# A hybrid decoder layer on one core: sixteen of the FFN's 22 inner tiles go through the down projection by seven block products, and small FFN operands move to PSUM

## The chip, the core and the metric

The kernel runs on one core of one Trainium2 chip. The metric is the device time in microseconds, as the median of several runs. Engines are named as in the profile: PE (matmul), PEld (its weight load), DVE (VectorE), ACT (ScalarE), POOL (GpSimd), SP (SyncE, which issues the DMAs here). Every engine works through its own queue in order.

## The reference, cut to what matters

The layer has a part that mixes tokens (three mixers, merged by gates) and a feed-forward part (FFN). The change lies in the FFN, with x of 1024 tokens by 1024 channels, D_FF = 2816, all float32:

```python
h = rms_norm(x, pre_ffn_norm)
u = causal_dwconv(h @ ffn_w_up, ffn_conv_w, ffn_conv_b)   # 1024 x 5632; three taps over time
gate, val = split(u)                                       # 2816 channels each
f = (gelu(gate, approximate=True) * val) @ ffn_w_down      # 2816 -> 1024
x = x + rms_norm(f, post_ffn_norm)
```

## The kernel before, in words

**Exact products by three matmuls.** Each float32 operand is kept as a rounded hi part (type fp32r) and the rest lo. A 128x128 block of weights times 128x512 of data is three matmuls: hi by hi, hi by lo, lo by hi. Making hi is a copy on ACT, making lo a subtraction on DVE or POOL. Data is channel by token: a tile has 128 channels and a half (512) of the tokens, h = 0 or 1.

**Seven block products.** Where a product is cut into 2x2 blocks, it can be made from seven products of sums of blocks in place of eight. The SSM part of the input projection and most of the up projection do this. `weights7` (L494 to L530) loads two tiles of 512 KB, makes the sums of weight blocks and splits them: four copies on ACT (L511, L520, L523, L525), eight operations on POOL (L512 to L526). `combos` makes the sums of the data blocks. `product` issues one of the seven, 12 matmuls.

**The FFN, up.** The FFN's 22 inner tiles are called f; each has a gate and a value tile (`u = 2f`, `2f+1`). The first `N_FIRST` = 4 are made plainly by halves in `up_half` (L1530), then `rhs` gets the sums of data blocks (L1571 to L1589), and 18 calls of `up_pair` (L1538) make one f each with 84 matmuls. Partial results collect in the PSUM banks x, y, z of a pool of six (`bank`); `snap` (L1512) copies the state of x to SBUF where a later step needs it. The second half of the value tile is the difference of two snapshots, s7 - s3, on POOL (L1555). `conv` runs the convolution over time in `E.conv` (L303 to L312): a scaled copy on ACT (L306), on DVE two shifted multiply-adds (L310) and, for h = 1, two narrow ones with the two columns at the edge kept from h = 0 (the `halo` tile, L308 and L312). GELU on ACT goes back into the gate's SBUF tile (L1524), `gated` (L1526) multiplies on DVE (L1527) and stores the tile to `m_d` in DRAM.

**The FFN, down.** `DOWN` lists six chunks of inner tiles: four, four, four, four, two, four. `m_split` (L1598) loads a tile of `m_d` into SBUF and splits it (ACT L1601, DVE L1602). `down` (L1604) does each of eight output tiles j by `fm_unit`, for both halves; the first chunk is copied to the 16 accumulator tiles `acc` by ACT (L1615), later ones are added by DVE (L1617). The last chunk is kept out of the loop: its weights and data are split ahead, and it is done column part by column part (`LAST`) with the final norm, the residual `x1` (two loads of 2 MB) and the output. The first chunk's splits are put into the last `up_pair` (`between`).

**Order.** A scheduler fixes each engine's order ahead of time from a model; tile pools make an instruction wait where a buffer is still in use. All loads and stores here are issued by SP in its order, so a load that waits for a buffer holds those behind it.

Of the kernel before, what the change touches and what calls it, by code (L numbers as in the profile page):

```python
# [33 lines left out]
C_ID, C_TI, C_MD, C_ME, C_TS, C_NT, C_SM = [128 * i for i in range(7)]  # L34
C_N = 8 * 128
# [57 lines left out]
def layout(a):  # L93
# [31 lines left out]
    for i, (c0, c1) in enumerate(TM_CHUNKS):  # L125
# [16 lines left out]

    dns = [units(dn[c * 128:(c + n) * 128], ar(DM)) for c, n in DOWN]
    out.update(
# [9 lines left out]
        wup=units(up, fch), **{f"wdn{i}": d for i, d in enumerate(dns)})  # L154
# [4 lines left out]
DOWN = [(0, 4), (4, 4), (8, 4), (12, 4), (16, 2), (18, 4)]  # L159
# [25 lines left out]
U_BUFS = 4  # L185
OSQ = 6

# [12 lines left out]
def trunk(ctx: ExitStack, tc: tile.TileContext, A: dict, outT: bass.AP, dbg=None):  # L200
# [24 lines left out]
    tab = cp.tile([128, C_N], F32, name="tab")  # L225
# [5 lines left out]
    ident = tab[:, C_ID:C_ID + 128]  # L231
    tri_i = tab[:, C_TI:C_TI + 128]
    rtab = cp.tile([128, 256], R32, name="rtab")
# [151 lines left out]
    nc.scalar.dma_start(ident, A["c_tab"][:, C_ID:C_ID + 128])  # L385
# [8 lines left out]
    nc.sync.dma_start(tab[:, 128:], A["c_tab"][:, 128:])  # L394
# [962 lines left out]
def tail_stage(nc, tc, es, env):  # L1357
# [49 lines left out]
    for n, (br_i, k0, nk, src) in enumerate(((2, 12, 4, "wb_nsa"), (1, 8, 4, "wb_sb"), (0, 0, 8, "wb_ssm"))):  # L1407
        if n == 2:
            yq = br.enter_context(tc.tile_pool(name="yq", side="right", reuse_waits="tile", bufs=8))
        ys = [load_y(k0 + k) for k in range(nk)]  # L1410
        for j in range(8):
            pss = fm_unit(psd, load_w(A[src][j], nk * 128), lambda k, h: ys[k][h], nk)
            e = (bt if n else E.bt0).tile([128, T], F32, name="ge")
            nc.sync.dma_start(e, E.g_d[(br_i * 8 + j) * 128:(br_i * 8 + j + 1) * 128, :])
            for h in range(2):
                b = e[:, hs(h)]
                d = b
                if n == 0:
                    d = part[h, j] = lo_t(F32)
                V.tensor_tensor(d, pss[h], b, op=OP.mult)  # L1420
                if n == 1:
                    P.tensor_tensor(part[h, j], part[h, j], b, op=OP.add)
                elif n == 2:
                    P.tensor_tensor(b, part[h, j], b, op=OP.add)
                    hi, lo = mix[h, j] = hi_t(), lo_t()
                    act(hi, b, AF.Copy)
                    V.tensor_tensor(lo, b, fl(hi), op=OP.subtract)
        if n == 0:
            E.both.close()
            E.st1.close()  # L1430
            psd = es.enter_context(tc.tile_pool(name="psd2", reuse_waits="tile", bufs=6, space=PSUM))
            psn = es.enter_context(tc.tile_pool(name="psn", reuse_waits="tile", bufs=2, space=PSUM))
# [74 lines left out]
    def bank():  # L1507
        return psd.tile([128, 512], F32, name="dense", tag="dense")

    def snap(ps):  # L1510
        s = up_.tile([128, 512], F32, name="snap", bufs=5)
        act(s, ps, AF.Copy)  # L1512
        return s

    m_d = E.scratch("m_d", [NFF * 128, T])

    def conv(u, h, ps, st):
# [19 lines left out]
    def up_pair(f, rhs, between=None):  # L1537

        st = {}
        w = E.weights7(wx, A["wup"][2 * f], A["wup"][2 * f + 1], 512)  # L1540
        x, y, z = bank(), bank(), bank()
        E.product(x, w, rhs, 1, True)
        s1 = snap(x)
        E.product(y, w, rhs, 2, True)
        V.tensor_tensor(y, y, s1, op=OP.add)
        conv(2 * f, 0, y, st)
        E.product(x, w, rhs, 6, False)
        s2 = snap(x)
# [6 lines left out]
        P.tensor_tensor(s7, s7, s3, op=OP.subtract)  # L1555
        E.product(z, w, rhs, 4, False)
        V.tensor_tensor(z, z, s2, op=OP.subtract)
# [14 lines left out]
    later = []  # L1572
    for k in range(4):
# [10 lines left out]
        later += [(5, k, t1, hi_t), (4, k, t4, lo_t)]  # L1584

    for q, k, t, place in sorted(later, key=lambda x: (-x[0], x[1])):
        rhs[q][k] = hi, lo = place(), x_t()
        act(hi, t, AF.Copy)
        V.tensor_tensor(lo, t, fl(hi), op=OP.subtract)  # L1589
# [3 lines left out]
    def m_tile(f, h, s):  # L1593
        t = x_t(F32) if s is None else up_.tile([128, 512], F32, name=f"u{s}")
        nc.sync.dma_start(t, m_d[f * 128:(f + 1) * 128, hs(h)])
        return t

    def m_split(f, h):  # L1598
        src = m_tile(f, h, None if f < DOWN[0][1] else f % 2)
        hi, lo = hi_t(), lo_t()  # L1600
        act(hi, src, AF.Copy)  # L1601
        V.tensor_tensor(lo, src, fl(hi), op=OP.subtract)  # L1602
        return hi, lo
# [4 lines left out]
    def down(ci, f0, nf, ms):  # L1608
        end = None
        for j in range(8):  # L1610
            pss = fm_unit(psd, load_w(A[f"wdn{ci}"][j], nf * 128), lambda k, h: ms[f0 + k, h], nf)
            for h, ps in enumerate(pss):
                a = acc[h][j]
                if ci == 0:
                    act(a, ps, AF.Copy)  # L1615
                else:
                    end = V.tensor_tensor(a, a, ps, op=OP.add)  # L1617
        return end
# [7 lines left out]
    tc.keep_in_program_order(nc.scalar.preload_act_table_set(E.TABLE))  # L1626
    for ci, (f0, nf) in enumerate(DOWN[:last]):
        if ci == 0:
            acc = [[x_t(F32) for _ in range(8)] for _ in range(2)]
        i = down(ci, f0, nf, m_chunk(f0, nf) if ci else ms0)  # L1630
        if ci == last - 2:
            late = i
# [5 lines left out]
    def w_split(j, place):  # L1638
        ws.append(load_w(A[f"wdn{last}"][j], 512, place, up_.tile([128, 512], F32, name="snap", bufs=5)))
# [17 lines left out]
    def norm_rows(ss, W):  # L1657
# [7 lines left out]
        rb = up_.tile([128, 512], F32, name="u1")  # L1665
# [15 lines left out]
    for s0, s1 in LAST:  # L1681
# [3 lines left out]
        ss = up_.tile([128, 512], F32, name="u0")  # L1685
        for j in range(8):
# [10 lines left out]
            else:  # L1697
                sq = up_.tile([128, 512], F32, name="snap", bufs=5)
# [24 lines left out]
```

## Time and profile before

| | us |
|---|---|
| median of three runs | 2294.1 |
| lowest and highest | 2286.16, 2295.38 |
| the profiled execution | 2297.28 |
| its span, first to last instruction | 2295.5 |
| mean granted clock of PE | 0.985 of full speed |

The span is the time from the first instruction to the last. The profile's times count from the span's start. The FFN's up projection begins shortly after 1600 us, and the down projection shortly after 2000. In a group of instructions, the columns are line, engine, operation, output and inputs by the program's names with their shapes, the count, then busy time in us, the mean of one in ns, and the idle time just before with what ended it. In a list of waits, the columns are who waited, for whom, and in us the total, the number of waits and the longest.

### The profile page before, as it was taken

The page shows a single profiled execution, that of the slowest core. Times are in us where ns is not written, and L with a number is a line of the kernel's source. Part 1 is how long each engine was busy: PE and PEld are TensorE (multiplying, and loading weights), DVE is VectorE, ACT ScalarE, POOL GpSimd, SP SyncE. Part 2 cuts the span into 40 slices and gives each one's busy share as a digit, 9 for nine tenths or more (in the row PEclk, how much of TensorE's full clock was granted, in tenths as well). Part 3 has the DMA queues.
Part 4 walks back from the last instruction along what each step waited for, and adds up shares of the span by engine and source line. Part 5 has one row for each costly group of instructions (what it writes and reads, how often), then busy time and mean ns, then how long its engine had stood idle before and what let it go on. Part 6 is the DMA issues. An engine that isn't in the chain of part 4 may idle for free.

```text
span 2295.5 us, 29758 instructions
## 1 busy us (share of the span) xinstructions
PE 2197.3 (96%) x10663; PEld 1755.3 (76%) x10663; DVE 1346.2 (59%) x2376; ACT 1164.9 (51%) x2185; POOL 1184.5 (52%) x853
## 2 busy tenths in 40 slices
PE   7999999998999999999999999999899999999997
PEld 7878889865665678878775678887678888878886
DVE  7765554268567526556536653359876777744346
ACT  6544443466756646667755421245545555553124
POOL 3676741246736733333347655446578888822213
PEclk9999999999999999999999999999999999999998
DMA  4233341320221011112253253334322222264212
GB/s 170 81 111 108 116 132 62 112 70 24 62 67 31 12 56 42 60 65 93 83 211 112 80 213 129 119 128 162 106 79 86 85 83 83 84 223 130 93 32 74
DMA packets 115349, 222.03 MB, mean 97 GB/s; under 512 B 28160, under 2 KB 42432, under 8 KB 115200
## 3 DMA queue, kind: packets, MB, share of 16 engines
q1 hardware_dynamic: 112608, 217.80, 28.0%
q10 hardware_dynamic: 2592, 2.32, 0.3%
q8 instruction: 84, 1.38, 0.2%
q14 instruction: 65, 0.53, 0.1%
HBM read 162.80 MB, written 57.28 MB: 96 GB/s over the span
## 4 chain that ended last, share of the span: by engine, by line
PE 77%; DVE 11%; ACT 5%; issue 3%; DMA 3%; POOL 2%; SPq 0%; DVEq 0%; ACTq 0%; POOLq 0%
PE dense L208 55%; PE ps_s L208 7%; PE ps_o L208 6%; PE ps_t L208 6%; PE ps_b L208 4%; POOL wlo L273 1%; DVE x L1484 1%; DVE mx L938 1%; DVE u L310 1%; DVE osq L1457 1%; DVE x L1589 1%; DMA wraw<-in_wdn 1%; DMA wraw<-in_wfm 0%; DVE x L1677 0%; DMA x<-in_xT 0%
## 5 line engine op out<-in xcount | busy, mean ns | idle before, releaser
L273 POOL TENSOR_TENSOR wlo<-wraw,whi 128x1024 fp32r<-128x1024 f32 (+2 forms) x134 | 266.5, 1989 | 444.1 <-ACT whi L272 435.4
L208 PE MATMUL dense<-hi,whi 128*128 128x512 f32 x816 | 308.2, 392 | 4.8 <-ACT whi L272 4.8
L208 PE MATMUL dense<-hi,wlo 128*128 128x512 f32 x752 | 289.3, 394 | 8.9 <-POOL wlo L273 7.9
L208 PE MATMUL dense<-lo,whi 128*128 128x512 f32 x688 | 269.3, 392 | 0.5 <-POOL lo L1497 0.5
L208 PE MATMUL dense<-h_hi,whi 128*128 128x512 f32 x656 | 263.8, 402 | 0.0
L208 PE MATMUL dense<-h_lo,whi 128*128 128x512 f32 x656 | 257.5, 393 | 0.0
L208 PE MATMUL dense<-h_hi,wlo 128*128 128x512 f32 x656 | 257.2, 392 | 0.0
L272 ACT ACTIVATE whi<-wraw 128x1024 fp32r<-128x1024 f32 (+2 forms) x134 | 116.1, 867 | 277.4 <-PE dense L208 228.8
L976 POOL TENSOR_TENSOR wT_lo<-wT,wT_hi 128x512 fp32r<-128x512 f32 x132 | 168.5, 1288 | 101.3 <-ACT wT_hi L975 93.2
L208 PEld LDWEIGHTS dense<-hi,whi 128*128 128x128 f32 x816 | 154.2, 189 | 39.5 <-ACT whi L272 6.9
L208 PE MATMUL dense<-x,uhi 128*128 128x512 f32 x552 | 177.3, 392 | 3.9 <-ACT x L584 2.4
L208 PEld LDWEIGHTS dense<-hi,wlo 128*128 128x128 f32 x752 | 142.1, 189 | 41.7 <-POOL wlo L273 10.4
L208 PEld LDWEIGHTS dense<-lo,whi 128*128 128x128 f32 x688 | 130.0, 189 | 28.6 <-POOL lo L1497 1.4
L208 PEld LDWEIGHTS dense<-h_hi,wlo 128*128 128x128 f32 x656 | 123.7, 189 | 26.7
L208 PEld LDWEIGHTS dense<-h_hi,whi 128*128 128x128 f32 x656 | 124.4, 190 | 23.8
L208 PEld LDWEIGHTS dense<-h_lo,whi 128*128 128x128 f32 x656 | 124.3, 189 | 22.5
L1180 POOL TENSOR_TENSOR s_lo<-sa,s_hi 128x512 fp32r<-128x512 f32 (+2 forms) x48 | 53.5, 1115 | 152.1 <-ACT s_hi L1179 152.1
L938 DVE TENSOR_REDUCE mx<-ps_t 128x1 f32<-128x384 f32 (+3 forms) x192 | 98.7, 520 | 47.7 <-PE ps_t L208 44.0
L208 PEld LDWEIGHTS dense<-x,uhi 128*128 128x128 f32 x552 | 103.7, 189 | 27.5 <-ACT x L584 3.6
L965 ACT ACTIVATE wT<-ps_s 128x512 f32<-128x512 f32 x132 | 78.4, 594 | 72.4 <-PE ps_s L208 67.1
L310 DVE SCALAR_TENSOR_TENSOR u<-dense,pv,u 128x510 f32<-128x510 f32 (+1 forms) x140 | 101.9, 737 | 7.8 <-ACT u L306 7.6
L521 POOL TENSOR_TENSOR ulo<-uf,uhi 128x1024 fp32r<-128x1024 f32 x30 | 72.5, 2418 | 63.4 <-ACT uhi L520 63.4
(514 smaller groups left out, 5690.9 us busy)
## 6 DMA issues: line engine op xcount, KB each, us to landing
wraw<-in_wfm SPq DMA_DIRECT2D x62, 512.0 KB, 3.7
wraw<-in_wup SPq DMA_DIRECT2D x52, 512.0 KB, 3.7
g_d<-gate_e SPq DMA_DIRECT2D x48, 256.0 KB, 2.1
s_d<-o SPq DMA_DIRECT2D x48, 256.0 KB, 2.0
ge<-g_d SPq DMA_DIRECT2D x24, 512.0 KB, 3.5
m_d<-u SPq DMA_DIRECT2D x44, 256.0 KB, 2.0
u<-m_d SPq DMA_DIRECT2D x36, 256.0 KB, 4.0
row<-s_d SPq DMA_DIRECT2D x16, 512.0 KB, 4.2
```

The lines of the kernel that those rows point to most:

```text
L208: i = f(*a, **k)
L272: act(hi, raw, AF.Copy)
L273: (V if tiles else P).tensor_tensor(lo, raw, fl(hi), op=OP.subtract)
L310: V.scalar_tensor_tensor(o[:, d:], ps[:, :512 - d], taps[d], o[:, d:], op0=OP.mult, op1=OP.add)
L521: P.tensor_tensor(l24, f24, fl(h24), op=OP.subtract)
L938: V.tensor_reduce(mx[:, h, a, n:n + 1], pm[:, :w], axis=AX, op=OP.max)
L965: act(w.rearrange("p h q -> p (h q)"), pz, AF.Exp)
L976: P.tensor_tensor(lo, wf, fl(hi), op=OP.subtract)
L1180: (P if SB_SLO else V).tensor_tensor(s_lo[:, c0:], a[:, c0:], fl(s_hi[:, c0:]), op=OP.subtract)
L1457: eng.tensor_tensor(sums[0], sums[0], sq, op=OP.add)
L1484: e.tensor_tensor(o[j], o[j], x, op=OP.add)
L1589: V.tensor_tensor(lo, t, fl(hi), op=OP.subtract)
```

## The change

1. **Down projection.** Tiles 0 and 1 are a plain first chunk (`down_first`, 96 matmuls), tiles 2 to 5 the plain last chunk; tiles 6 to 21 go by seven products in four chunks of four tiles (`DOWN7`), each for two halves d of the output columns: eight units of 84 matmuls. A unit (`down7`) takes its weights from `weights7`, uses all six banks, and after each of 14 groups of six matmuls DVE adds or subtracts a bank into one accumulator tile. Banks go on collecting after they were read.
2. **Its data.** For f of 6 and up, `gated` keeps tiles of two neighbouring f, and `combine` makes four sums on DVE in the next `up_pair` (two calls of `deferred`). The seven operands go to DRAM (`m7_d`) in place of `m_d`. Each chunk loads and splits 14 of them (`m_sets`), 56 in all; most have the loaded tile copied to PSUM by ACT, so that DVE's subtraction takes one operand from there (`by_psum`). The load goes into the lo tile itself.
3. **Up projection.** The halo columns stand in a PSUM bank; GELU writes to the PSUM bank of the convolution's input, and the gating reads it there. Product 4 has a bank of its own (`v`); `z - s2` and `z - s3` are made in place in PSUM by DVE, and POOL's L1555 is gone, as is one snapshot.
4. **Room.** Constant tables get a pool of their own that is closed with the mixers; `u0`, `u1` and `snap` have 6, 2 and 6 buffers (before 4, 4 and 5). The pool `wx`, where `weights7` works, stays in use to the end of the seven-product units; `x1` is loaded into its place.

Counted in the two programs: matmuls of 128x512 with a moving operand of that size 7414 before, 7318 after; DVE two-input operations 1095 and 1235; ACT activations 2111 and 2166; POOL's 741 and 755; DMAs issued by SP 678 and 710.

```diff
-DOWN = [(0, 4), (4, 4), (8, 4), (12, 4), (16, 2), (18, 4)]
+DOWN7 = [6, 10, 14, 18]
+DOWN = [(0, 2), (2, 4)]
...
     def conv(u, h, ps, st):
         s = u % 2
         if h == 0:
-            st["halo", s] = up_.tile([128, 4], F32, name="halo", bufs=12)
-        st[s, h] = up_.tile([128, 512], F32, name=f"u{s}")
+            st["halo", s] = halos[:, 4 * (u % 16):4 * (u % 16) + 4]
+        st[s, h] = up_.tile([128, 512], F32, name=f"u{s}", bufs=(U0_BUFS, U1_BUFS)[s])
         E.conv(st[s, h], h, ps, [pvc(PV_FW, 3 * u + 2 - d) for d in range(3)], pvc(PV_FB, u), st["halo", s])
         if s == 0:
-            act(st[0, h], st[0, h], AF.Gelu_apprx_tanh)
+            act(ps, st[0, h], AF.Gelu_apprx_tanh)
+            st["gelu", h] = ps
+    halos = psn.tile([128, 512], F32, name="psn", tag="psn")
...
     def gated(f, h, st):
-        V.tensor_tensor(st[0, h], st[0, h], st[1, h], op=OP.mult)
-        nc.sync.dma_start(m_d[f * 128:(f + 1) * 128, hs(h)], st[0, h])
+        m = st[0, h]
+        V.tensor_tensor(m, st["gelu", h], st[1, h], op=OP.mult)
+        if not in_pairs(f):
+            nc.sync.dma_start(m_d[f * 128:(f + 1) * 128, hs(h)], m)
+            return
...
+        if f % 2 and h:
+            later.extend(combine(p, even[0], even[1], st[0, 0], m))
...
+    def combine(p, b11, b12, b21, b22):
+        t7, t6, t4 = [up_.tile([128, 512], F32, name="snap", bufs=SNAPS) for _ in range(3)]
+        def one():
+            V.tensor_tensor(t7, b12, b22, op=OP.subtract)
+            V.tensor_tensor(b12, b11, b12, op=OP.subtract)
+            for q, t in ((7, t7), (5, b12)):
+                nc.sync.dma_start(m7_rows(p, q), t)
+        def two():
+            V.tensor_tensor(t6, t7, b11, op=OP.subtract)
+            V.tensor_tensor(t4, t6, b21, op=OP.add)
+            for q, t in ((6, t6), (4, t4)):
+                nc.sync.dma_start(m7_rows(p, q), t)
+        return one, two
...
         x, y, z = bank(), bank(), bank()
+        v = psn.tile([128, 512], F32, name="psn", tag="psn")
...
         conv(2 * f, 0, y, st)
+        deferred()
...
         E.product(z, w, rhs, 7, True)
-        s7 = snap(z)
+        V.tensor_tensor(s2, z, s2, op=OP.subtract)
         E.product(x, w, rhs, 5, False)
         s3 = snap(x)
-        P.tensor_tensor(s7, s7, s3, op=OP.subtract)
-        E.product(z, w, rhs, 4, False)
-        V.tensor_tensor(z, z, s2, op=OP.subtract)
-        conv(2 * f + 1, 0, z, st)
+        E.product(v, w, rhs, 4, True)
+        V.tensor_tensor(v, v, s2, op=OP.add)
+        conv(2 * f + 1, 0, v, st)
+        V.tensor_tensor(z, z, s3, op=OP.subtract)
         gated(f, 0, st)
+        deferred()
         E.product(x, w, rhs, 3, False)
-        conv(2 * f + 1, 1, s7, st)
+        conv(2 * f + 1, 1, z, st)
...
+    def split_to(hi, lo, src, by_psum=False):
+        nc.sync.dma_start(fl(lo), src)
+        whole = fl(lo)
+        if by_psum:
+            whole = psn.tile([128, 512], F32, name="psn", tag="psn")
+            act(whole, fl(lo), AF.Copy)
+        act(hi, fl(lo), AF.Copy)
+        V.tensor_tensor(lo, whole, fl(hi), op=OP.subtract)
+        return hi, lo
...
+    def m_sets(c):
+        sets = [{}, {}]
+        for n, q in enumerate(ORDER7):
+            for i, st in enumerate(sets):
+                if (2 * c + i) % 3 == 2 and n < 5:
+                    hi, lo = x_t(), x_t()
+                else:
+                    hi, lo = hi_t(), lo_t()
+                st[q] = split_to(hi, lo, m7_rows(2 * c + i, q), c > 0 or i == 1)
+        return sets
...
+    def down7(c, sets, w0=None):
+        def product2(ps, q, n, first):
+            hi, lo = w[q]
+            for k in range(2):
+                s = slice((2 * n + k) * 128, (2 * n + k + 1) * 128)
+                b = sets[k][q]
+                for m, (x, y) in enumerate(((hi, b[0]), (hi, b[1]), (lo, b[0]))):
+                    mm(ps, x[:, s], y, start=first and k == 0 and m == 0, stop=k == 1 and m == 2,
+                       skip_group_check=True)
+        end = None
+        for d in range(2):
+            w = weights(c, d) if d or c else w0
+            x, y, z = [[bank(), bank()] for _ in range(3)]
+            for q, ps, start, h, m, op in ((1, x, True, 0, 0, OP.add), (2, y, True, 0, 0, OP.add),
+                                           (6, x, False, 0, 1, OP.subtract), (7, z, True, 1, 1, OP.add),
+                                           (5, x, False, 1, 1, OP.subtract), (4, z, False, 0, 1, OP.add),
+                                           (3, x, False, 1, 0, OP.add)):
+                for n in range(2):
+                    product2(ps[n], q, n, start)
+                    a = acc[h][4 * d + 2 * n + m]
+                    end = V.tensor_tensor(a, a, ps[n], op=op)
+        return end
...
     for f in range(N_FIRST, NFF):
         up_pair(f, rhs, (lambda: ms0.update(m_chunk(*DOWN[0]))) if f == NFF - 1 else None)
+    while later:
+        deferred()
     tc.keep_in_program_order(nc.scalar.preload_act_table_set(E.TABLE))
+    w7 = weights(0, 0)
+    sets = m_sets(0)
+    down_first(*DOWN[0], ms0)
+    for c in range(len(DOWN7)):
+        if c:
+            sets = m_sets(c)
+        end = down7(c, sets, w7)
+        if c == 2:
+            late = end
```

More of the change, by code (lines that the diff above doesn't have):

```diff
@@ L1510, in snap @@
     def snap(ps):
-        s = up_.tile([128, 512], F32, name="snap", bufs=5)
+        s = up_.tile([128, 512], F32, name="snap", bufs=SNAPS)
         act(s, ps, AF.Copy)
@@ L1591, in tail_stage, with split_in @@
     acc = []
[L1593 to L1596, printed above, removed]
-    def m_split(f, h):
[L1599 to L1603, printed above, removed]
+    def split_in(src):
+        hi, lo = hi_t(), lo_t()
+        return split_to(hi, lo, src)
@@ L1605, in m_chunk, with down_first @@
     def m_chunk(f0, nf):
         return {(f, h): m_split(f, h) for h in range(2) for f in range(f0, f0 + nf)}
[L1608 to L1609 removed]
+    def down_first(f0, nf, ms):
+        n = nf * 128
         for j in range(8):
[L1611 to L1618 removed]
+            raw = E.wp.tile([128, 1024], F32, name="wraw", bufs=2)[:, :n]
+            nc.sync.dma_start(raw, A["wdn0"][j])
+            hi, lo = [up_.tile([128, n], R32, name=f"f{x}", bufs=2) for x in ("hi", "lo")]
+            act(hi, raw, AF.Copy)
+            P.tensor_tensor(lo, raw, fl(hi), op=OP.subtract)
+            pss = fm_unit(psd, (hi, lo), lambda k, h: ms[f0 + k, h], nf)
+            for h, ps in enumerate(pss):
+                a = x_t(F32)
+                acc[h].append(a)
+                act(a, ps, AF.Copy)
@@ L1638, in w_split @@
     def w_split(j, place):
-        ws.append(load_w(A[f"wdn{last}"][j], 512, place, up_.tile([128, 512], F32, name="snap", bufs=5)))
+        ws.append(load_w(A[f"wdn{last}"][j], 512, place, up_.tile([128, 512], F32, name="snap", bufs=SNAPS)))
     for k in range(nf):
@@ L1697, in tail_stage @@
             else:
-                sq = up_.tile([128, 512], F32, name="snap", bufs=5)
+                sq = up_.tile([128, 512], F32, name="snap", bufs=SNAPS)
                 act(sq[:, :W], a, AF.Square)
```

68 lines of the change are left out of this document (48 added, 20 removed).

## The prediction

> **What bounds the kernel now.** I read the page's busy line first, then the shares of the chain that ended last, then the busy time of each engine by stage.
>
> ```profile
> PE 2197.3 (96%) x10663; PEld 1755.3 (76%) x10663; DVE 1346.2 (59%) x2376; ACT 1164.9 (51%) x2185; POOL 1184.5 (52%) x853
> PE 77%; DVE 11%; ACT 5%; issue 3%; DMA 3%; POOL 2%; SPq 0%; DVEq 0%; ACTq 0%; POOLq 0%
> PE dense L208 55%; PE ps_s L208 7%; PE ps_o L208 6%; PE ps_t L208 6%; PE ps_b L208 4%; POOL wlo L273 1%; DVE x L1484 1%; DVE mx L938 1%; DVE u L310 1%; DVE osq L1457 1%; DVE x L1589 1%; DMA wraw<-in_wdn 1%; DMA wraw<-in_wfm 0%; DVE x L1677 0%; DMA x<-in_xT 0%
> ```
>
> PE is busy for 96% of the span and makes 77% of the chain. But the change touches the FFN alone, so the stages decide (each row: stretch; its length; then busy time and instructions of PE, PEld, DVE, ACT, POOL; granted clock; DMA share; GB/s):
>
> ```profile
> core 0: us, PE busy (x) PEld busy (x) DVE busy (x) ACT busy (x) POOL busy (x), PEclk, DMA share, GB/s
> 1600.00:1700.00 100.00, 85.99 (x352) 66.49 (x351) 86.25 (x113) 49.86 (x71) 59.20 (x26) 0.96 0.31 109
> 1700.00:2000.00 300.00, 300.00 (x1318) 248.06 (x1317) 208.42 (x279) 156.17 (x223) 252.70 (x144) 1.00 0.24 82
> 2000.00:2065.00 65.00, 59.52 (x253) 48.10 (x252) 35.07 (x56) 30.92 (x51) 22.21 (x15) 0.97 0.60 206
> 2065.00:2233.00 168.00, 168.00 (x743) 139.16 (x742) 68.49 (x102) 43.71 (x78) 40.56 (x34) 1.00 0.28 88
> 2233.00:2295.00 62.00, 46.92 (x307) 42.53 (x305) 40.82 (x88) 26.51 (x57) 18.23 (x19) 0.90 0.19 68
> ```
>
> 1600 to 1700 holds the first four inner tiles of the up projection and the making of the operands for its seven products; 1700 to 2000 the pairs by seven products; 2000 to 2065 the change from up to down; 2065 to 2233 the plain down projection; the rest the last chunk's end and the final norm. In the second and fourth stretch PE never stops: 168.00/743 = 0.226 us per matmul. At that rate the first stretch does 352 x 0.226 = 79.6 us of work in 100, so 20.4 are lost there, and the third 57.2 in 65, so 7.8 are lost.
>
> **Fewer matmuls, the sure part.** Sixteen of 22 inner tiles were 16 x 8 x 2 x 3 = 768 matmuls of 128x512. Now they are four chunks x two halves of the columns x seven products x two outputs x two tiles x three = 672. The program loses exactly 96 matmuls, all where PE is busy without a gap: **96 x 0.226 = -21.7 us**, if the other engines keep pace.
>
> **Do the new units keep pace?** There are eight units of 84 matmuls, 19.0 us of PE each. Each has one preparation of weights (the same helper as in an up pair), 14 adds of a PSUM bank to the accumulators, and, with two units to a chunk's 14 splits, seven splits. The prices:
>
> ```profile
> 1800.00:1900.00 100.00, 100.00 (x443) 82.81 (x442) 69.63 (x95) 52.25 (x76) 84.29 (x48) 1.00 0.24 82
> L1617 DVE TENSOR_TENSOR x<-x,dense 128x512 f32<-128x512 f32 x64 | 43.9, 687 | 86.6 <-PE dense L208 86.5
> L1602 DVE TENSOR_TENSOR lo<-u,hi 128x512 fp32r<-128x512 f32 x36 | 25.1, 737 | 27.6 <-ACT hi L1601 27.6
> L1601 ACT ACTIVATE hi<-u 128x512 fp32r<-128x512 f32 x36 | 21.3, 627 | 5.8 <-DMA u<-m_d 2.9 <-PE dense L208 2.4
> L523 ACT ACTIVATE uhi<-uf 128x1024 fp32r<-128x1024 f32 x18 | 19.1, 1060 | 3.7 <-PE dense L208 3.6
> L525 ACT ACTIVATE ahi<-wraw 128x512 fp32r<-128x512 f32 x18 | 11.4, 632 | 19.3 <-PE dense L208 19.3
> L1555 POOL TENSOR_TENSOR snap<-snap 128x512 f32<-128x512 f32 x18 | 23.7, 1319 | 9.0 <-ACT snap L1512 9.0
> u<-m_d SPq DMA_DIRECT2D x36, 256.0 KB, 4.0
> ```
>
> The first row is 443/84 = 5.27 up pairs with 84.29/5.27 = 16.0 us of POOL each; less the 1.3 of L1555, the weights cost POOL 14.7. DVE in a unit: 14 x 0.69 + 7 x 0.74 = 14.8 us. ACT: three wide copies and one narrow one for the weights, 3.8, and for most splits two copies (the hi part, and the whole tile to PSUM, so that DVE's subtraction has one operand in SBUF), 7 x 1.25 = 8.8; together 12.6. All lie under 19.0, so on averages the units stay PE's.
>
> What averages hide is order. A unit takes all six banks of its pool. Most banks return after at least one other product, 12 matmuls or 2.7 us, but the last product ends in the banks that the next unit starts with: PE has only the other half of that product, 6 x 0.226 = 1.4 us, for an add of 0.69. A split of 0.74 just ahead of that add takes the slack, and a split that waits for its DMA (4.0 us issue to landing) holds all adds behind it, as DVE runs its queue in order. The loads themselves stand on SP's queue behind weight loads, which wait for buffers that POOL frees. Nothing in the old trace has this mix. Lower bound 0 (the up pairs run at 100% with the same weights), upper bound 30 (a landing time of 4.0 at nearly each of eight unit starts). I take **+4**, half a us per unit start: DVE's 14.8 of 19.0 leaves room to be ahead.
>
> **Up pairs.** Removed or cheapened per pair, on DVE and POOL; added: the combinations of gated tiles.
>
> ```profile
> L310 DVE SCALAR_TENSOR_TENSOR u<-snap,pv,u 128x510 f32<-128x510 f32 x16 | 44.8, 2797 | 0.0
> L310 DVE SCALAR_TENSOR_TENSOR u<-dense,pv,u 128x510 f32<-128x510 f32 x46 | 33.8, 735 | 0.0
> L312 DVE SCALAR_TENSOR_TENSOR u<-halo,pv,u 128x2 f32<-128x2 f32 x31 | 35.8, 1156 | 0.0
> L312 DVE SCALAR_TENSOR_TENSOR u<-halo,pv,u 128x1 f32<-128x1 f32 x31 | 12.2, 394 | 0.0
> L1557 DVE TENSOR_TENSOR dense<-dense,snap 128x512 f32<-128x512 f32 x16 | 11.2, 699 | 11.3 <-PE dense L208 11.3
> ```
>
> The same shape takes 2.80 us from SBUF and 0.74 from PSUM, so the odd tile's convolution saves 2.1; the halo edges, two of each size per pair, 3.1 together, fall to about 0.8 (0.2 each, below the shorter row); two more adds of 0.70 come in. DVE goes from 69.63/5.27 = 13.2 to about 10.2 us a pair. The combinations, four for each two inner tiles, so two a pair, cost between 0.69 (L1617) and 2.80 each: 11.6 to 15.8 of 19.0. POOL loses its 1.3. PE held 100% before and the load is no heavier: **0**. The fourth bank for product 4 (v) is used once a pair. If this cover were gone, the 18 pairs would bring 18 times the excess, but it is 3 us away.
>
> **First four tiles.** The halo edges and the gating go to PSUM here too.
>
> ```profile
> L312 DVE SCALAR_TENSOR_TENSOR u<-halo,pv,u 128x1 f32<-128x1 f32 x8 | 9.4, 1181 | 0.0
> POOL wlo L273 <- ACT whi L272: 35.1, 10, 6.0
> PE dense L208 <- POOL wlo L273: 4.6, 2, 4.2
> 1640.00:1650.00 10.00, 6.57 (x19) 5.28 (x20) 10.00 (x15) 3.35 (x6) 6.24 (x2) 0.66 0.30 105
> ```
>
> DVE saves some 8 us of its 86 (eight at 1.18 go to about 0.2), and it was full from 1640 to 1650. But PE's longest wait there names the weight split on POOL, and that waited for ACT. Bounds 0 and -8; I take **-1.5**, nearer to the waits than to DVE's load.
>
> **The change from up to down.** Before, 7.8 us were lost here:
>
> ```profile
> PE dense L208 <- ACT snap L1512: 3.0, 1, 3.0
> PE dense L208 <- ACT whi L272: 2.3, 1, 2.3
> ```
>
> Afterwards more has to happen. The first plain chunk is two tiles: 96 matmuls, 21.7 us. Beside it ACT has 16 accumulator copies, eight weight copies, the first unit's weights (3.8) and 14 splits, half of them with a second copy:
>
> ```profile
> L1615 ACT ACTIVATE x<-dense 128x512 f32<-128x512 f32 x16 | 9.4, 590 | 7.9 <-PE dense L208 7.8
> L272 ACT ACTIVATE whi<-wraw 128x256 fp32r<-128x256 f32 x8 | 3.3, 416 | 18.1 <-PE dense L208 16.3 <-issue 1.8
> L1589 DVE TENSOR_TENSOR x<-x,lo 128x512 fp32r<-128x512 f32 x4 | 10.2, 2596 | 0.0
> ```
>
> That is 9.4 + 3.3 + 3.8 + 14 x 0.63 + 7 x 0.63 = 29.7 us of ACT, due by the last product of the first unit, some 21.7 + 16 = 38 us on. It fits, with no slack for the start: GELU of the last pair, its gating, two to four combinations, their DMAs out and the loads back (SP issues the new loads behind those stores). I take 13 lost in place of 7.8, **+5**; bounds 0 (ACT fits) and +12 (seven subtractions here have both operands in SBUF while POOL makes the weights, and such ones took 2.60 in place of 0.74: 7 x 1.9 = 13).
>
> The Trainium skill, "SBUF — State Buffer", section "SBUF: two separate sides", says that a DVE operation with two SBUF inputs and a GpSimd operation that reads SBUF exclude each other for a whole instruction. The 2.80 against 0.74 above agrees; by that rule the sum would take the upper bound here, +12 for +5.
>
> **The tail.** The last plain chunk has four tiles as before. The 4 MB of x1 are now loaded after the last seven-product unit, not in 2000 to 2065:
>
> ```profile
> x<-x_d SPq DMA_DIRECT2D x2, 2048.0 KB, 13.1
> ```
>
> Two x 13.1 = 26 us lie beside a last chunk whose PE work alone is 192 x 0.226 = 43 us; the first half is wanted after 96 matmuls (21.7 us) and a norm. Cost **0** (up to +3). What is won is the bandwidth in the transition (206 GB/s there, 0.60 of the DMA engines): down to -3, in the bounds above.
>
> **Sum.** -21.7 + 4 + 0 - 1.5 + 5 + 0 = -14.2 us. The profiled execution took 2297.3 (span 2295.5 and 1.8 around it) and would take 2283.1; it stood 3.2 above the median of 2294.1, so against that median: **2280 us**.
>
> **Rivals.**
> 1. *Given back at the transition and at the units' starts.* DVE's SBUF subtractions take 2.6 us beside POOL and the loads stand behind weight loads. Transition +12, units +8, first tiles 0: -1.7, **2292**. For it: seven of the first 14 subtractions and up to four combinations around the handover read SBUF twice. Against: PE's slack in the first plain chunk.
> 2. *Slower: the splits hold the adds.* DVE's order is fixed before the run, and 56 splits stand among 112 adds. If each keeps PE from a bank by one DVE operation (0.7 us), 56 x 0.7 = 39 us are lost in place of the 4: 2280 + 35 = **2315**. It decides from (21.7 + 1.5 - 5)/56 = 0.33 us a split. For it: the six banks all in use and DMA's 4.0 us in DVE's path. Against: 14.8 of 19.0 us.
> 3. *A larger gain.* If the first tiles do hang on DVE (-8) and the transition gets no worse since weights and x1 are out of its way (0), with units at +2: -27.7, **2266**.
>
> That the change does not remove work is no rival: the matmuls are counted in the program.
>
> **How the numbers follow.** Forecast (2270 to 2288) 0.46, rival 1 0.24, rival 2 0.19, rival 3 0.11. The range 2262 to 2302 holds the forecast, rivals 1 and 3, and the milder part of rival 2 (half of whose 35 gives 2298). Half a per cent, 11.5 us, is about what a measurement of this kernel can tell from no change; the bound 2282.6 cuts the forecast's own range, leaving about a fifth of it on the other side. Faster: 0.11 + 0.39 = 0.50. Same: 0.07 + 0.24 + a little of rival 2 = 0.33. Slower: 0.17.
>
> **What would show it.** PE at 100% in the eight units with some 96 fewer matmuls in the stage; DVE near 15 of each 19 us there; halo rows (L312) at 0.2 to 0.4 us; the conv from a snapshot gone; fewer than 13 us lost between the last up pair and the first unit. Wrong if PE waits in the units name a split or its DMA, if the transition loses over 15 us, or if a combination takes 2.7 us and an up pair leaves 19.0.

## The result, and the profile after

The changed kernel took 2276.2 us (median of four runs, 2272.9 to 2278.7) against 2291.5 for the kernel before (four runs): a ratio of 0.9934, 95% interval 0.9907 to 0.996. Timed again beside its variants it took 2271.5 (six runs) against 2290.5 (18 runs): 0.9921, 0.9904 to 0.9939. So 15 to 19 us were won. The profiled execution took 2275.59 with a span of 2273.8.

The busy line of the changed kernel's page, then its stages, with the columns of the table of before:

```profile
PE 2178.6 (96%) x10567; PEld 1735.5 (76%) x10567; DVE 1383.3 (61%) x2516; ACT 1202.1 (53%) x2240; POOL 1211.9 (53%) x867
```

```profile
1600.00:1700.00 100.00, 88.53 (x349) 68.67 (x348) 84.53 (x117) 49.51 (x70) 59.69 (x30) 0.93 0.31 100
1700.00:2000.00 300.00, 298.94 (x1318) 246.90 (x1317) 197.08 (x345) 149.56 (x208) 218.04 (x126) 1.00 0.29 98
2000.00:2065.00 65.00, 59.16 (x253) 46.66 (x252) 42.34 (x67) 42.21 (x74) 34.77 (x25) 1.00 0.67 224
2065.00:2233.00 168.00, 166.95 (x742) 137.84 (x741) 121.83 (x179) 86.98 (x139) 89.49 (x51) 1.00 0.39 128
```

PE has 96 records fewer, as the program says, and its share is unchanged. From 2065 on DVE, ACT and POOL work about twice as much as before (1.8 to 2.2 times), and PE still loses only one microsecond of 168. From 2000 to 2065 the busy time looks as before, which will turn out to be chance.

A fixed window shows different work in two kernels. So I counted along PE's order of instructions and cut both traces at the same matmuls. B runs from the second half of the first four tiles to 98 matmuls before the end of the up projection; D is the first 96 matmuls of the down projection (in the changed kernel 88 of the first plain chunk and eight of the first unit), E the rest up to the last chunk. PE's pace is the 0.2267 us per matmul at which it works where nothing holds it. Microseconds:

| stretch | before | after | difference |
|---|---|---|---|
| A: all ahead of the second half of the first tiles | 1622.0 | 1623.1 | +1.1 |
| B: that half, and the pairs but the last 98 matmuls | 383.4 | 380.7 | -2.8 |
| C: the last 98 matmuls of the up projection (22.2 at PE's pace) | 27.2 | 27.6 | +0.4 |
| D: 96 matmuls (21.8 at PE's pace) | 21.8 | 24.5 | +2.8 |
| E: 768 matmuls before (174.1), 672 after (152.3) | 177.1 | 153.9 | -23.2 |
| F: the last chunk and the norm, to the end | 64.0 | 64.0 | 0.0 |

The sum is -21.7. In E, the 96 matmuls are -21.8, the new units lose 1.6 where none was lost before, and 3.0 that the old second chunk lost are gone. Stretch A, which the change hardly touches, took 1616.0 to 1624.5 in the five profiled executions of this study that I cut so. That spread is larger than the 3 to 6 us by which the profiled pair's difference stands off the medians'. (In the kernel before, `up_pair` begins at line 1539 and `down` at 1608, not at 1538 and 1604.)

Four stretches of a unit's 19 us between 2091 and 2186 (the same columns):

```profile
2091.00:2110.00 19.00, 19.00 (x85) 15.73 (x85) 10.14 (x15) 7.89 (x12) 13.51 (x8) 1.00 0.43 137
2129.00:2148.00 19.00, 19.00 (x86) 15.67 (x85) 16.47 (x28) 14.08 (x25) 12.30 (x9) 1.00 0.47 152
2148.00:2167.00 19.00, 19.00 (x86) 15.73 (x85) 15.61 (x21) 10.28 (x17) 15.72 (x9) 1.00 0.41 127
2167.00:2186.00 19.00, 17.95 (x78) 14.28 (x77) 17.39 (x24) 6.96 (x11) 11.97 (x7) 1.00 0.31 101
```

Only the last of these has a hole in PE, and there DVE is at 17.4 of 19. The groups behind it, from 1590 us to the end, with the count, busy us, mean ns and the idle time ahead:

```profile
L326 DVE SCALAR_TENSOR_TENSOR u<-psn,pv,u 128x2 f32<-128x2 f32 x44 | 9.2, 209 | 0.0
L1717 DVE TENSOR_TENSOR x<-x,dense 128x512 f32<-128x512 f32 x112 | 73.8, 681 | 34.3 <-PE dense L219 34.2
L1675 DVE TENSOR_TENSOR lo<-psn,hi 128x512 fp32r<-128x512 f32 x39 | 26.5, 684 | 5.3 <-ACT hi L1674 3.5 <-ACT psn L1673 1.7
L1675 DVE TENSOR_TENSOR lo<-lo,hi 128x512 fp32r<-128x512 f32 x19 | 20.3, 1070 | 7.8 <-ACT hi L1674 7.7
L1587 DVE TENSOR_TENSOR snap<-snap,u 128x512 f32<-128x512 f32 x8 | 16.2, 2027 | 0.0
```

The wider halo edges (128x2) fell from 0.93 (in the pairs 1.16) to 0.21 us. A split with one operand in PSUM takes 0.68, with two in SBUF 1.07. All four operations of a combination have two SBUF operands; the means of the four run from 0.68 to the 2.03 us of the fourth (L1587), about the prediction's 0.69 to 2.80.

### The profile page after: what moved, and what is told of

Read it like the earlier page. It is cut to its first block, busy times and chain, and to the rows that moved or that the text cites. A ratio compares the mean times of both kernels' runs of the same rounds, so it can differ in the third digit from the quotient of the medians.

```text
span 2273.8 us, 29870 instructions
## 1 busy us (share of the span) xinstructions
PE 2178.6 (96%) x10567; PEld 1735.5 (76%) x10567; DVE 1383.3 (61%) x2516; ACT 1202.1 (53%) x2240; POOL 1211.9 (53%) x867
## 4 chain that ended last, share of the span: by engine, by line
PE 73%; DVE 12%; ACT 5%; issue 4%; DMA 3%; POOL 3%; SPq 0%; DVEq 0%; ACTq 0%; POOLq 0%
PE dense L219 49%; PE ps_s L219 7%; PE ps_o L219 6%; PE ps_t L219 5%; PE ps_b L219 4%; PE psn L219 2%; DVE u L324 1%; DVE osq L1472 1%; DVE x L1499 1%; DVE mx L952 1%; DMA lo<-m_d 1%; DMA wraw<-in_wfm 1%; DVE lo L1514 1%; DVE x L1659 1%; POOL wlo L526 0%
## 5 line engine op out<-in xcount | busy, mean ns | idle before, releaser
L287 POOL TENSOR_TENSOR wlo<-wraw,whi 128x1024 fp32r<-128x1024 f32 (+1 forms) x94 | 212.7, 2263 | 299.1 <-ACT whi L286 294.4
L219 PE MATMUL dense<-hi,whi 128*128 128x512 f32 x576 | 214.7, 393 | 0.5 <-ACT whi L286 0.5
L219 PE MATMUL dense<-hi,wlo 128*128 128x512 f32 x512 | 201.8, 397 | 7.9 <-POOL wlo L287 5.8
L219 PE MATMUL dense<-x,uhi 128*128 128x512 f32 x600 | 191.5, 392 | 2.3 <-ACT x L598 2.3
L219 PE MATMUL dense<-lo,whi 128*128 128x512 f32 x448 | 176.7, 394 | 1.8 <-DVE lo L1514 1.8
L286 ACT ACTIVATE whi<-wraw 128x1024 fp32r<-128x1024 f32 (+1 forms) x94 | 92.5, 984 | 160.9 <-PE dense L219 130.6
L535 POOL TENSOR_TENSOR ulo<-uf,uhi 128x1024 fp32r<-128x1024 f32 x38 | 92.2, 2427 | 114.6 <-ACT uhi L534 112.7
L219 PEld LDWEIGHTS dense<-h_hi,whi 128*128 128x128 f32 x656 | 124.0, 189 | 23.6
L219 PEld LDWEIGHTS dense<-hi,whi 128*128 128x128 f32 x576 | 109.3, 190 | 25.1 <-ACT whi L286 1.2
L324 DVE SCALAR_TENSOR_TENSOR u<-dense,pv,u 128x511 f32<-128x511 f32 (+1 forms) x140 | 103.5, 741 | 33.7 <-ACT u L320 33.6
L219 PEld LDWEIGHTS dense<-hi,wlo 128*128 128x128 f32 x512 | 97.2, 190 | 31.4 <-POOL wlo L287 8.1
L538 POOL TENSOR_TENSOR ulo<-uf,uhi 128x1024 fp32r<-128x1024 f32 x38 | 92.2, 2427 | 36.4 <-ACT uhi L537 32.5
```

Source lines behind the costliest of these rows:

```text
L219: i = f(*a, **k)
L286: act(hi, raw, AF.Copy)
L287: (V if tiles else P).tensor_tensor(lo, raw, fl(hi), op=OP.subtract)
L324: V.scalar_tensor_tensor(o[:, d:], ps[:, :512 - d], taps[d], o[:, d:], op0=OP.mult, op1=OP.add)
L535: P.tensor_tensor(l24, f24, fl(h24), op=OP.subtract)
L538: P.tensor_tensor(l31, f31, fl(h31), op=OP.subtract)
```

## The experiments

My theory after the result: PE bounds the FFN, the 96 matmuls come off it, the units have cover. The rivals: the gain comes from the operands in PSUM, which unload DVE; or the splits in DVE's order still take part of it.

**The changed kernel again**, with no edit, as the measure for the others.

> The changed kernel once more, timed beside its variants on the same chip. My theory: the 96 matmuls, 21.7 us, come off a PE that is busy without a gap, and some 2 us are given back in the new units, so 0.990 to 0.994 of the kernel before. If the earlier profile, 21.7 us shorter in span, was a lucky one and most of the gain is given back, 0.994 to 0.998.

2271.5 us, 0.9921 (0.9904 to 0.9939), in the middle of the theory's range.

**The plain down projection with the changed up projection.**

```diff
-DOWN7 = [6, 10, 14, 18]
-DOWN = [(0, 2), (2, 4)]
+DOWN7 = []
+DOWN = [(0, 4), (4, 4), (8, 4), (12, 4), (16, 2), (18, 4)]
...
-        return DOWN7[0] <= f < DOWN7[-1] + 4
+        return False
...
-        end = down7(c, sets, w7)
+        i = down(ci, f0, nf, m_chunk(f0, nf) if ci else ms0)
```

> The changed up projection (halo columns, GELU, gating and product 4 in PSUM) with the plain down projection of the kernel before, no combinations and no seven-product units. Theory, the gain is the 96 matmuls: PE's 21.7 us are back, the 1.6 us lost in the units go, so the kernel before's time within 4 us (ratio 0.998 to 1.002). Rival, the PSUM operands bring the gain by unloading DVE: the time of the changed kernel, ratio 0.992 to 0.995.

2287.7 us (12 runs), 0.9989 (0.998 to 0.9998). So the seven-product down projection itself is worth 2287.7 - 2271.5 = 16.2 us, and the theory holds. (By stretches C to E of the two profiles it is 218.8 - 206.0 = 12.8; the intervals of the two ratios allow both.) But 96 matmuls are 21.8, so 5.6 or more are given back, more than the 1.6 of the units. The stages of this run say where: the change from up to down, first the kernel before, then this one.

```profile
2000.00:2032.00 32.00, 28.96 (x121) 23.43 (x120) 24.03 (x36) 15.29 (x25) 15.78 (x10) 0.95 0.34 112
2032.00:2056.00 24.00, 24.00 (x108) 19.87 (x107) 10.18 (x18) 12.38 (x20) 5.14 (x4) 1.00 0.81 278
2056.00:2080.00 24.00, 21.56 (x94) 17.23 (x93) 6.69 (x10) 12.65 (x23) 5.24 (x4) 1.00 0.71 247
```

```profile
2000.00:2032.00 32.00, 32.00 (x142) 26.39 (x141) 24.84 (x42) 19.06 (x32) 11.90 (x9) 1.00 0.56 182
2032.00:2056.00 24.00, 24.00 (x107) 19.89 (x106) 6.79 (x14) 11.54 (x20) 4.98 (x4) 1.00 0.83 284
2056.00:2080.00 24.00, 24.00 (x107) 19.88 (x107) 7.49 (x11) 12.82 (x24) 6.39 (x5) 1.00 0.54 156
```

With the changed up projection and a plain down projection PE does not stop at all there: by the matmuls, 22.3 us for the 98 of C against 27.2, and 0.0 lost in the first chunks against 3.0. So two things stand against each other in the changed kernel. The changed up projection takes the old loss away, 4.9 + 3.0 us, and the seven-product path brings a new one: in C 27.6 - 22.2 = 5.3 (before rounding) and in D 2.8, together 8.1. One thing does not fit: from stretch B on, this run's profile is 9.0 us shorter than that of the kernel before, its median only 2.8 (0.5 to 4.6). There is one profile of the kernel before, so how much of the 7.9 each of its executions loses stays open.

**The residual's load held back, in the kernel before.**

```diff
+    for n in ("uf0", "uf1", "uhi", "ulo", "wraw"):
+        t = wx.tile([128, 1024], F32 if n[1] in "fr" else R32, name=n, bufs=1 if n[1] in "fr" else 2)
+        act(t[:, :1], acc[1][7][:, :1], AF.Copy)
     wx_.close()
```

> The kernel before, with x1's two loads of 2 MB held back until the fourth down chunk is added up (five tiny ACT copies into the place that x1 takes); nothing else changed. Theory, those loads delayed the first down chunk's weights (one landed after 11.9 us) and cost PE the 2.4 us gap at the chunk's second unit: 2 to 3 us less than the kernel before, and PE at 100% after the last up pair. Rival, ACT's queue is the cause and the weight would be late anyway: no change within 1 us.

The time alone does not tell: 0.9997 (0.9985 to 1.0008). The trace does:

```profile
2056.00:2080.00 24.00, 24.00 (x107) 19.88 (x106) 6.41 (x10) 13.16 (x24) 5.82 (x5) 1.00 0.49 160
```

107 matmuls where the kernel before did 94; the gap is gone, by matmuls 3.0 us in that stretch. So x1's loads were the cause of that gap, and 3 us are below what these medians show. In the run before this one x1 is loaded there as well (from 2036.7) and PE does not stop; why the load costs nothing there was not tested.

**The small operands of the up projection back in SBUF.**

```diff
-            st["halo", s] = halos[:, 4 * (u % 16):4 * (u % 16) + 4]
+            st["halo", s] = up_.tile([128, 4], F32, name="halo", bufs=12)
...
-            act(ps, st[0, h], AF.Gelu_apprx_tanh)
-            st["gelu", h] = ps
+            act(st[0, h], st[0, h], AF.Gelu_apprx_tanh)
+            st["gelu", h] = st[0, h]
...
-    halos = psn.tile([128, 512], F32, name="psn", tag="psn")
```

> The changed kernel with the halo columns, the GELU result and so the gating's first operand back in SBUF; all else kept. Theory, DVE's load in an up pair is covered: it rises from about 12.5 to 15 us of the 19.0 that PE needs, PE stays at 100% in the pairs, and the first four tiles lose up to 3 us more; 0 to +3 us over the changed kernel. Rival, the combinations fit only because the other operands moved to PSUM: each of the 18 pairs runs over by 1 us, +18 us, and PE falls below 100% between 1720 and 2000 us.

2327.5 us, 1.0166 (1.0148 to 1.0184): 56 us more than the changed kernel. Neither size was right, and my theory of cover by sums fell. From 1700 to 2000 us, this run's stage, its longest wait of PE and the groups behind it:

```profile
1700.00:2000.00 300.00, 276.36 (x1159) 223.32 (x1158) 239.14 (x296) 126.43 (x179) 192.81 (x110) 0.96 0.25 84
```

```profile
PE dense L219 <- ACT snap L1527: 23.6, 13, 4.7
```

```profile
L326 DVE SCALAR_TENSOR_TENSOR u<-halo,pv,u 128x1 f32<-128x1 f32 x28 | 39.3, 1403 | 0.0
L326 DVE SCALAR_TENSOR_TENSOR u<-halo,pv,u 128x2 f32<-128x2 f32 x27 | 39.2, 1452 | 0.0
L1542 ACT ACTIVATE u<-u 128x512 f32<-128x512 f32 x26 | 16.5, 633 | 63.2 <-DVE u L326 62.8
```

1159 matmuls in place of 1318 are 36 us lost in this stretch alone. 23.6 of them are these waits; most of the rest is PE working at a lower granted clock after the long ones (after the wait of 4.0 us shown below 12 matmuls in 5 us, at a clock of 0.50). DVE is busy for 239 of 300, that is 17.3 us a pair at 84/1159 of the stretch's 300 = 21.7: below PE's 19.0. Not its sum but its order does it. The time line shows a whole chain through four queues (first a GELU on ACT, then DVE, SP, ACT again and PE; idle time ahead in brackets; in SP's first row the second of two stores ends at 1783.47):

```profile
1781.30 1.29 ACT L1542 ACTIVATE u<-u 128x512 f32<-128x512 f32 x2 [7.10 <-DVE u L326]
1781.96 1.15 DVE L1557 TENSOR_TENSOR u<-u,u 128x512 f32<-128x512 f32 x1
1771.48 11.99 SPq L1568 DMA_DIRECT2D m_d<-u  x2
1785.04 0.44 SPq L520 DMA_DIRECT2D wraw<-in_wup  x1
1790.74 0.63 ACT L539 ACTIVATE ahi<-wraw 128x512 fp32r<-128x512 f32 x1 [4.02 <-DMA wraw<-in_wup]
1792.22 1.06 ACT L1527 ACTIVATE snap<-dense 128x512 f32<-128x512 f32 x2
1792.85 0.80 PE L219 MATMUL dense<-hi,uhi 128*128 128x512 f32 x1 [3.99 <-ACT snap L1527]
```

Both GELUs wait 7.1 us for the narrow edge operation on DVE, and the gating on DVE (L1557) comes after them. SP holds the store of the gated tile until then, and the loads of the next weights stand behind that store. ACT waits 4.0 us for the second load, the snapshots stand behind that copy in ACT's queue, and PE's next product into the snapshot's bank stands behind the snapshot. Of the 13 waits of PE in this stretch nine, 22.5 of the 23.6 us, come just after ACT has waited 3.6 to 7.8 us for such a load; in the changed kernel ACT waits for no load in this stretch. Only three short ones, 0.8 us together, are for a snapshot that stands directly behind a late GELU. POOL read the weights before these until 1782.57, so how early the loads could have gone without the store is not shown.

**The halo columns alone back in SBUF.** 
```diff
-            st["halo", s] = halos[:, 4 * (u % 16):4 * (u % 16) + 4]
+            st["halo", s] = up_.tile([128, 4], F32, name="halo", bufs=12)
...
-    halos = psn.tile([128, 512], F32, name="psn", tag="psn")
```

> The changed kernel with the halo columns alone back in SBUF; GELU and gating stay in PSUM. With all three back, PE waited in the pairs for snapshots on ACT, which stood behind GELUs that waited for DVE's narrow edge operations (1.40 and 1.45 us each in place of 0.21). Theory, the edges are the larger part of DVE's extra time (4 x 1.2 = 4.9 us a pair against 1.6 for the gating): 30 to 50 of those 56 us over the changed kernel. Rival, it is the GELU's round through SBUF and the gating: under 15 us.

2304.4 us, 1.0066 (1.0046 to 1.0086): some 33 us over the changed kernel, by the ratios too. The edges are the larger part, as expected, and here too ACT waits for the weight loads (12 times, 57.4 us in all from 1700 to 2000).

**Without the combinations.** The plain down projection of above with all three operands in SBUF.

> The plain down projection (no combinations, no seven-product units) with the halo columns, GELU and gating back in SBUF; product 4 in its own bank and the subtractions on DVE as changed. Theory, it is the combinations on top of the SBUF operands that broke the pairs: without them DVE has 15.5 us a pair, PE stays near 100% there, and the time is within 10 us of the plain down projection with PSUM operands (2288). Rival, moving the subtraction from POOL to DVE breaks them already: 30 us or more over it.

2332.2 us, 1.0189 (1.0171 to 1.0207), 44 us over the plain down projection with PSUM operands (46 by the ratios). The rival's price came, 30 us or more: it is not the combinations. With SBUF operands, the changed up pair (product 4 in its own bank, both subtractions and the addition on DVE) no longer keeps PE busy, even with the old down projection; ACT waits for the weight loads as above (10 times, 60.1 us). The pair of before had those SBUF operands too, but POOL made one subtraction and DVE stood idle for 4 us in a pair I looked at. Which of the up pair's other edits broke it, the numbers of buffers among them, was not separated, so the move of the subtraction is not shown to be the cause.

**All splits from SBUF.**

```diff
-                st[q] = split_to(hi, lo, m7_rows(2 * c + i, q), c > 0 or i == 1)
+                st[q] = split_to(hi, lo, m7_rows(2 * c + i, q))
```

> The changed kernel with every split's subtraction taken from SBUF (no ACT copy of the whole tile to PSUM): 49 ACT copies fewer, 49 DVE subtractions with two SBUF operands more. A unit's DVE work is 14 adds of 0.68 and seven splits at 1.07 (the mean of the 19 such splits in the changed kernel) to 2.09 us (a long one of them): 17.0 to 24.2 of PE's 19.0. Theory, the units have cover: splits near 1.1, 0 to +5 us over the changed kernel. Rival, beside POOL's 13.5 us per unit they take 2 us each: DVE becomes the bound, 5 us for each of eight units, +40 us, and POOL's weight chain gets longer too.

2283.7 us (10 runs), 0.9971 (0.9961 to 0.998): 7 to 12 us over the changed kernel's two measurements, between the two expectations.

```profile
L1675 DVE TENSOR_TENSOR lo<-lo,hi 128x512 fp32r<-128x512 f32 x58 | 65.0, 1133 | 16.5 <-ACT hi L1674 16.4
```

```profile
PE dense L219 <- DVE x L1717: 6.0, 9, 1.0
```

From the first plain chunk's last matmul to the start of the units' last add, this run took 163.7 us, the changed kernel 155.3. The splits cost 1.13 us each, not 2; PE waits nine times for an add, at most 1.0 us. This is the second rival's mechanism at work, at a fifth of its price. The Trainium skill, "SBUF — State Buffer", section "SBUF: two separate sides", has a DVE operation with two SBUF inputs and a GpSimd one that reads SBUF exclude each other for a whole instruction. The trace agrees: 29 of the 58 splits began while POOL worked on an operation and took 1.58 us on average, the other 29 began between two and took 0.69; for the 23 that took over 1.0 us, the time is what was left of that operation plus 0.55.

**The subtraction of 49 splits done twice.**

```diff
-        V.tensor_tensor(lo, whole, fl(hi), op=OP.subtract)
+        for _ in range(1 + by_psum):
+            V.tensor_tensor(lo, whole, fl(hi), op=OP.subtract)
```

> The changed kernel with the subtraction of the 49 splits that go through PSUM done twice (0.68 us more of DVE each, 4.2 a unit): DVE goes from 14.3 to 18.5 us of a unit's 19.0. Theory, DVE's order costs nothing as long as its sum is below PE's: 0 to +6 us. Rival, the splits stand in order ahead of adds for banks that PE waits for, so each extra operation delays PE: 49 times 0.68, +33 us.

2276.5 us, 0.995 (0.9932 to 0.9968), within the theory's 0 to 6. The same stretch took 155.5 us against 155.3. 4.2 us more of DVE in each unit cost PE next to nothing.

**Without the splits of three chunks.**

```diff
-        if c:
-            sets = m_sets(c)
```

> The changed kernel without the loads and splits of chunks two to four: their products use the first chunk's data again, so 42 loads, 84 to 91 ACT copies and 42 DVE subtractions are left out and the output is not the reference's. Theory, the splits are hidden but for the one hold of 1.1 us seen in the units: 1 to 2 us less than the changed kernel, PE at 100% in all eight units. Rival, the splits hold the adds: 6 us or more come off.

2271.1 us, 0.9919 (0.9901 to 0.9937); the same stretch took 153.9 us, 1.4 less. All splits together cost the units about that much.

**Fewer copies, and more copies, at the change from up to down.** 
```diff
-                st[q] = split_to(hi, lo, m7_rows(2 * c + i, q), c > 0 or i == 1)
+                st[q] = split_to(hi, lo, m7_rows(2 * c + i, q), c > 0)
```

and, in the other kernel,

```diff
-                st[q] = split_to(hi, lo, m7_rows(2 * c + i, q), c > 0 or i == 1)
+                st[q] = split_to(hi, lo, m7_rows(2 * c + i, q), True)
```

> The changed kernel, but the seven splits of the second pair of tiles in the first chunk subtract from SBUF, without ACT's copy of the whole tile to PSUM: seven ACT copies of 0.59 us fewer at the change from up to down. Theory, the loss there (8.1 us by matmuls not done) is ACT's, since PE's waits name snapshots and weight copies on ACT: 1 to 3 us less than the changed kernel. Rival, DVE's subtractions from SBUF beside POOL take 2.1 us in place of 0.68 and hold the adds and convolutions: 2 to 6 us more.

> The changed kernel with the last seven splits (the first pair of tiles of the first chunk) also copied to PSUM by ACT, so that no split of a seven-product chunk has two SBUF operands. Theory by DVE: seven subtractions fall from 1.07 or more to 0.68, and the long ones beside POOL go: 1 to 4 us less than the changed kernel. Rival by ACT: seven copies of 0.59 us more in a stage where ACT is busy for 5.9 of 6 us, 2 to 5 us more.

Fewer: 2279.7 us, 0.9948 (0.9929 to 0.9967), so the second expectation held, and the longest wait for a snapshot there is 5.9 us in place of 2.3. Ahead of it GELU waits 5.85 us for DVE, where two splits from SBUF took 4.3 us together, and what stands on ACT behind that GELU, the snapshot among it, comes that much later. More: 2271.0, 0.9921 (0.9906 to 0.9936), the changed kernel's own time; neither expectation came. So these seven copies are not what holds PE there; nor did seven cheaper subtractions gain anything that the medians show.

**The first unit's weights put later.**

```diff
-    w7 = weights(0, 0)
-    sets = m_sets(0)
     down_first(*DOWN[0], ms0)
+    w7 = weights(0, 0)
+    sets = m_sets(0)
```

> The changed kernel with the first unit's weights and the first chunk's splits put behind the first plain chunk in the order that the scheduler is given. Theory, the 8 us lost at the change from up to down come from the weights' POOL chain and the new splits beside the last pair: DVE's SBUF subtractions took 1.7 to 2.1 us beside POOL, GELU waited for DVE and the snapshots behind GELU held PE. Without them there PE loses 3 us or less up to the first plain chunk, if the first unit's start does not then wait for its weights: 3 to 6 us less than the changed kernel (2265 to 2269). Rival, the weights come too late for the first unit: 14.7 us of POOL work late by 5 or more, 2275 or more.

2275.9 us, 0.9948 (0.993 to 0.9966). Both were half right: up to the first plain chunk's end 2.4 us are lost in place of 8.1 (1.3 in C, 1.1 in D), and in E 9.3 in place of 1.6. PE's waits at the change, the changed kernel from 2000 to 2100 us, then this run from 1690 on:

```profile
PE dense L219 <- ACT snap L1527: 3.9, 3, 2.3
PE dense L219 <- ACT fhi L1729: 1.7, 2, 1.2
```

```profile
PE dense L219 <- ACT uhi L534: 6.2, 1, 6.2
PE dense L219 <- ACT snap L1527: 1.4, 2, 0.8
```

The waits for snapshots go, and one of 6.2 us for the unit's weights takes their place. No variant beat the changed kernel beyond its interval.

## Why the prediction was right, and where its steps were not

- **96 x 0.226 = -21.7: right.** PE has 96 records fewer, all in a stretch where it runs without a gap, and undoing this part alone brings back 16.2 us of time after the losses below.
- **Units, +4: the mechanism right, the size too large.** 1.6 us measured, of which 1.1 is one wait for an add (L1717). My half a us at every unit start was not needed: twice the DVE work on splits changed the units by less than 1 us. Rival 2 (2315) is excluded; beyond that one wait its mechanism shows only where splits have two SBUF operands, +8.4 us.
- **Up pairs, 0: right for the change, wrong in its reason.** "It is 3 us away" took DVE's sum as the measure of cover. With SBUF operands DVE's sum rises only to 17.3 of 19.0 and PE loses over 2 us a pair. What holds PE there is a chain through four queues: the edge operations on DVE make GELU and the gating late, SP holds the weight loads behind the gated tile's store, and ACT waits for the weights with the snapshot behind them. The edits whose worth I put at 0 are what lets this pair run at PE's pace: 56 us hang on them.
- **First four tiles, -1.5:** stretch B gave -2.8 in the first profile and -0.6 in the second one. Over all nine profiles with the three operands in PSUM B has a mean of 381.6, in the two with the old up projection 383.3: -1.7. Right as far as this can be told.
- **From up to down, +5: +0.2 in the trace, and for a reason that I did not have.** I forecast 13 lost in place of 7.8, as the old loss with an addition. Measured are 8.1 in place of 7.9, and none of the old loss stayed: 4.9 go with the changed up pair and 3.0 with the x1 load (the bound of -3 that I gave for it). The 8.1 are new, and that the two are nearly equal is luck. Two of its waits can be followed in these rows of the changed kernel, DVE first and then ACT:

```profile
2018.20 2.09 DVE L1675 TENSOR_TENSOR lo<-lo,hi 128x512 fp32r<-128x512 f32 x1
```

```profile
2021.96 0.60 ACT L1542 ACTIVATE dense<-u 128x512 f32<-128x512 f32 x1 [3.73 <-DVE u L326]
2022.50 0.58 ACT L1527 ACTIVATE snap<-dense 128x512 f32<-128x512 f32 x1
2024.68 1.14 ACT L1674 ACTIVATE hi<-lo 128x512 fp32r<-128x512 f32 x2
2025.72 0.76 ACT L320 ACTIVATE u<-psn,pv 128x512 f32<-128x512 f32 x1
2026.38 0.61 ACT L1674 ACTIVATE hi<-lo 128x512 fp32r<-128x512 f32 x1
2026.90 1.04 ACT L534 ACTIVATE uhi<-uf 128x1024 fp32r<-128x1024 f32 x1
2027.85 0.58 ACT L1527 ACTIVATE snap<-dense 128x512 f32<-128x512 f32 x1
```

  A split from SBUF takes 2.09 us, the edge operations come behind it, GELU waits 3.7 us for them, the snapshot follows GELU; PE's wait for that snapshot is 0.8 us. The longest wait, 2.3 us, is for the snapshot at 2027.85, and there ACT's own queue is full: the last thing ahead of it is the copy of the first unit's weights (L534). In the run that puts the unit's weights and splits later, three split copies stand ahead of this snapshot too, L534 does not, and PE has no such wait. So most of the 8.1 is the preparation of the first unit, set among the last pair's work: without it there 2.4 are left. Put later it costs PE 6.2 us at the unit's start, so no variant removes the loss. What part the splits and what part the weights have was not separated.
- **Tail, 0:** 64.0 us before and after.

So 2280 lies near 2276 and 2271 because the misses, the units by 2.4 and the change from up to down by 4.8, are small beside the sure term; both made the forecast too slow. Some of the nearness is luck. The 2280 starts from 2294.1, and later medians of the kernel before are 2.6 and 3.6 lower. And the terms that came true at the change and in the units (0.2 and 1.6) are nearer to rival 3's 0 and 2 than to mine; only its -8 for the first tiles did not come. Rival 1's +12 and +8 did not come either.

## What to carry to other kernels

Take the certain gain from the stretch where the bound engine has no gap, and then look for what it gives back at the borders of that stretch. Cover is not a sum of busy time: follow who waits for whom through each in-order queue, that of the DMA issues included, and ask what stands behind a waiting instruction. A new loss of the same size as one that it replaces looks in the profile like no change; undoing one part at a time tells them apart.

## What the runs showed of the hardware

A narrow DVE operation of 128x1 or 128x2 with two operands in SBUF took 1.40 and 1.45 us on average while POOL worked beside it (1700 to 2000 us of the run with the small operands in SBUF), and 0.21 with one of them in PSUM in the changed kernel. In the same stretch of the kernel before, the 16 of shape 128x1 that began between two POOL operations took 0.21 us and the 15 that began during one 0.59; the 31 of 128x2 all began during one and took 1.16. All but two of these narrow operations that began during one, in both runs, ended within 0.02 us of its end: the price is what is left of POOL's operation, not the size of DVE's own. And stretch A varied by 8.5 us between the five executions named above, so edits worth 3 us were seen in the trace and not in the medians.
